# Output projection and second feed-forward moved to token-major groups with seven products for eight

## The chip, the cores and the metric

The kernel runs on one core of a Trainium2 chip. The metric is the time of one execution in device microseconds (us). TensorE (PE) multiplies, VectorE (DVE), ScalarE (ACT) and GpSimd (POOL) do the rest, and SyncE (SP) issues the loads.

## What is computed

Two transformer blocks in float32 on 256 tokens of width 2048. The first mixes two attentions, multiplies by `w_out`, and has a gated feed-forward (FFN) of inner width 5632. The second runs gated linear attention beside differential attention, multiplies by `w_o`, and has an FFN with a causal convolution over three tokens. Cut to what the change touches:

```python
h = h + mixed @ w_out
hn = rmsnorm(h, ffn_norm)
h = h + (silu(hn @ w_gate) * (hn @ w_up)) @ w_down
x = rmsnorm(h, final_norm)                        # the second block's input
m = token_mixer(rmsnorm(x, attn_pre_norm))        # ends with o @ w_o
x = x + rmsnorm(m, attn_post_norm)
up = rmsnorm(x, ffn_pre_norm) @ w_ffn_in          # 2048 -> 2 * 5632
a, b = up[..., :5632], up[..., 5632:]
a = conv3(a) + conv_b                             # three taps over tokens
f = (gelu(a) * b) @ w_ffn_out
out = x + rmsnorm(f, ffn_post_norm)
```

## The kernel before

Every product is made of split operands: a float32 value is cut into a high part (ACT copies and rounds, line L471 for weights) and a low part (DVE subtracts, L475), and high·high, high·low and low·high are summed in PSUM. Weights stream through SP (L421) in pieces of 128x1024; a few pieces are held split ahead of use (`look`).

There are two forms of product.

- **Channel-major** (`group_w`, `mm_w`, L513 to L517): the weight tile stands in the array, the 256 tokens move. For each 128x128 weight tile there is one matmul of 512 columns (high weight, the tokens' high and low parts side by side) and one of 256 columns (low weight). I call the two a pair. The result has channels on the partitions.
- **Token-major** (`group_t`, L597): 128 tokens stand, 512 weight columns move, three matmuls of 512 columns per product. The result has tokens on the partitions. Here two pairs of k-tiles (k-tile: 128 rows of the weight) are not multiplied in the eight block products that two pairs of tiles need but in seven, of sums of blocks (Winograd's form of Strassen's scheme). The roles are B11, B22, t1, t3, t2, B21, t4; t1, t3, t2, t4 need a weight piece that DVE adds together first (L453), and t1, t3, t2 and B22 use sums of activation blocks (`combos`). The other k-tiles (`std`) are multiplied as usual. After t4, `early` sums four PSUM banks (`sums`, L634 to L638); at the end `late` adds the other four.

Before the change the first block's `w_out` (2 groups), gate and up (11 groups) and `w_down` (6 groups in three parts) are token-major, from `block1_out` and `block1_ffn`. The second block's `w_o` (`block2_out`) and its FFN (`block2_ffn`) are channel-major: 256 pairs for `w_o`, 1408 for the first FFN matrix, 704 for the second.

At the end of `block1_ffn` the residual is transposed on PE eight blocks at a time (`turned`, L668), and for each block ACT and DVE make the split operand (L503, L504), ACT makes two squares for the two norms' statistics (L699), which POOL sums (L709), and ACT copies the residual (L1192). `block2_out` collects the statistics of the norm after `w_o` the same way; `norm_now` turns them into a factor by matmuls against ones, and then DVE and POOL scale and add 16 tiles (L1492, L1493), from which the operand of the FFN is split (L503, L504). In `block2_ffn`, `act` turns each pair of FFN columns into an operand: halves summed (L676, L679), scaled (L685), convolved (L1512, L1513, L1515), gelu (L1517), product (L1520), split (L500, L501). The end is a norm over channels again, 16 tiles and 16 stores (L1553 to L1555).

Order: the program is written as one stream of groups with side tasks. `tick` counts the estimated time of the matmuls issued, and every 2400 ns `pump` lets each side task (a generator) go one `yield` further. A layer under the kernel then sets each engine's final order; each engine runs its own in order. A token-major group calls `finish(*tasks)` ahead of t2, since the side task's transposes use the bank that t2 will use:

```python
if op == "t2":
    self.finish(*tasks)
...
if op == "t4" and not left["t2"]:
    early(b)
    self.one = self.map[ROLES["t3"]]
```

Of the kernel before, what the change touches and what calls it, by code (L numbers as in the profile page):

```python
# [17 lines left out]
P = 128  # L18
# [9 lines left out]
PARTS = ((0, 15), (15, 15), (30, 14))  # L28
PARTS_T = ((0, 16), (16, 16), (32, 12))
# [3 lines left out]
DOWN_PAIRS = ((0, 1), (2, 3))  # L33
UCOLS = 2048
# [27 lines left out]
def group_order(npairs, rest):  # L62

    rest, out = list(rest), []
# [10 lines left out]
def weight_plan():  # L75
# [13 lines left out]
    def tgroup(key, w, kts, pairs, col):  # L89
# [5 lines left out]
        c2 = [(col + 512, col + 1024)] if isinstance(w, str) else c1  # L95
# [9 lines left out]
        orders[key] = group_order(len(pairs), rest)  # L105
# [40 lines left out]
    for p, (i0, n) in enumerate(PARTS_T):  # L146
# [15 lines left out]
    for g in range(8):  # L162
        group(("wo", g), "w_o_2", list(range(8, 16)) + list(range(8)), [(256 * g, 256 * g + 256)])
    for p, (i0, n) in enumerate(PARTS):
        for i in range(i0, i0 + n):
            for c in range(2):
                kts = list(range(8 * c, 8 * c + 8))
                ra, rb = [(128 * i, 128 * i + 128)], [(FF + 128 * i, FF + 128 * i + 128)]
                unit(("fi", i, c), ("w_ffn_in_2", kts, ra + rb))
        for g in range(8):  # L170
            group(("fo", p, g), "w_ffn_out_2", range(i0, i0 + n), [(256 * g, 256 * g + 256)])
# [119 lines left out]
class Prog:  # L291
# [69 lines left out]
    def tmp(self, tag="tmp", bufs=6):  # L361
        return self.ring.tile([P, S], F32, tag=tag, name=tag, bufs=bufs)
# [267 lines left out]
    def sums(self, b):  # L630

        nc = self.nc
        e, v, w, c = [self.fz.tile([P, 512], F32, tag="ft", name="ft", bufs=4) for _ in range(4)]
# [5 lines left out]
        return e, w, v, c  # L639
# [4 lines left out]
    def residual(self, h, g):  # L644

        nc = self.nc
        at = [h[t][:, 1024 * g + 512 * m:1024 * g + 512 * m + 512] for t in range(2) for m in range(2)]

        def early(b):
            for a, x in zip(at, self.sums(b)):  # L650
# [6 lines left out]
        return early, late  # L657

# [89 lines left out]

    def norm_now(self, acc, last, n, first, warm=(0, 0, 0)):


        nc = self.nc
        ss = self.bank("ms")
        sq = self.square(last)
        if warm[0]:
            self.keep_warm(warm[0])
        for i, a in enumerate((acc, sq)):
            for t in range(2):
                nc.tensor.matmul(ss[:, t:t + 1], a[:, t * P:t * P + P], self.ones[:, 0:1],
                                 start=(i == 0 and t == 0), stop=(i == 1), skip_group_check=True)  # L760
        r = self.rsqrt(self.mean_eps(ss[:, 0:2], n))
        if warm[1]:
            self.keep_warm(warm[1])
        b = self.bank("ms")
        rB = self.bcast(r, bank=b, first=lambda: [
            nc.vector.tensor_tensor(x, x, b[:, :S], op=ALU.mult) for x in first])
        if warm[2]:
            self.keep_warm(warm[2])
        return rB
# [130 lines left out]
    def block1_mix(self):  # L900
# [175 lines left out]
        for j in range(16):  # L1076
# [13 lines left out]
            for a, b in OUT_PAIRS:  # L1090
                if j == b:
                    cm.append(self.combos(gates[a][0], za, self.cbp))
        return mixed, cm

    def block1_out(self, mixed, cm):
# [6 lines left out]
        ss = self.hp.tile([P, 2, 4], F32, name="ss")  # L1102

        def done(j, src):
            hn.append(self.hl(src, self.col("ffn_norm", j)))
            for i, p in enumerate(GU_PAIRS):
                if j in p:
# [3 lines left out]
                    if all(k in xg for k in p):  # L1111
                        cs.append(self.combos(xg[p[0]], xg[p[1]], self.hp))

        task = None
        for g in range(2):
            early, late = self.residual(h, g)
            self.group_t(("out", g), mixed, cm, OUT_PAIRS, early, late, [task] if task else ())
            for t in range(2):
                for m in range(2):
                    at = slice(1024 * g + 512 * m, 1024 * g + 512 * m + 512)  # L1120
# [556 lines left out]
```

## Time and profile before

| what | value |
|---|---|
| median of 3 runs | 2526.42 us (2525.63 to 2526.6) |
| the profiled execution's own time | 2526.12 us |
| its span in the profile | 2524.3 us |
| PE busy | 2485.4 us, 98% |
| DVE busy | 1842.0 us, 73% |
| ACT busy | 1372.8 us, 54% |
| POOL busy | 118.2 us, 5% |
| moved by DMA | 458.46 MB, 182 GB/s on average |

The span is what the profiler saw of the program; the execution's own time lies 1.8 us above it. A busy PE is not a PE at its best: matmuls overlap, and a matmul's shown length (some 390 ns for 512 columns) is longer than the step from one to the next. So counts of matmuls in a stretch of time say more than busy shares.

### The profile page before, as it was taken

The numbers are of one execution on the slowest core, as the hardware profiler recorded it, in microseconds if no ns is written. First come the engines' busy times: TensorE is split into PE (matmuls) and PEld (weight loads), VectorE is DVE, ScalarE is ACT, GpSimd is POOL, SyncE is SP. The second block draws the span as 40 slices with busy tenths as digits, with TensorE's granted clock in tenths as the row PEclk, the third lists the DMA queues.
The fourth block names the chain that finished last, engine by engine and source line by source line (L and its number), as shares of the span: only waits on it lengthen the run. The fifth ranks groups of instructions, "written<-read, shape, count | busy, mean of one in ns | idle before, by whom it ended". The sixth has DMA issues, their size and how long they took to land.

```text
span 2524.3 us, 35146 instructions
## 1 busy us (share of the span) xinstructions
PE 2485.4 (98%) x13218; PEld 2128.2 (84%) x13218; DVE 1842.0 (73%) x2617; ACT 1372.8 (54%) x2036; POOL 118.2 (5%) x134
## 2 busy tenths in 40 slices
PE   9999999999999999999999999999999999999997
PEld 8988888888788888888888888887888888888886
DVE  8766775888887878878786677666876567656765
ACT  6555565556555455545465545555655455545553
POOL 3000000000000000000012000013000000000002
PEclk9999999999999999999999999999999999999998
DMA  6644555566556565656555544464555555555552
GB/s 235 200 159 142 167 176 184 188 212 199 193 183 208 184 205 179 201 188 206 182 184 163 187 158 151 144 203 146 175 188 183 193 189 190 183 191 191 187 174 92
DMA packets 131723, 458.46 MB, mean 182 GB/s; under 512 B 14624, under 2 KB 17056, under 8 KB 131296
## 3 DMA queue, kind: packets, MB, share of 16 engines
q1 hardware_dynamic: 130608, 452.78, 54.7%
q10 hardware_dynamic: 944, 3.43, 0.4%
q8 instruction: 103, 1.69, 0.3%
q14 instruction: 68, 0.56, 0.1%
HBM read 454.06 MB, written 2.10 MB: 181 GB/s over the span
## 4 chain that ended last, share of the span: by engine, by line
PE 94%; DVE 4%; ACT 1%; issue 1%; POOL 0%; DMA 0%; POOLq 0%; SPq 0%; ACTq 0%; DVEq 0%
PE acc L516 33%; PE q L597 30%; PE acc L517 17%; PE acc L514 3%; PE acc L549 2%; PE acc L548 2%; PE acc L550 2%; PE acc L513 1%; PE ms L789 1%; DVE wl L475 1%; PE tr L668 1%; DVE hl L504 1%; PE ms L1337 1%; PE ms L818 1%; ACT wh L471 0%
## 5 line engine op out<-in xcount | busy, mean ns | idle before, releaser
L475 DVE TENSOR_TENSOR wl<-raw,wh 128x1024 fp32r<-128x1024 f32 (+4 forms) x939 | 1116.1, 1196 | 499.8 <-ACT wh L471 495.8
L471 ACT ACTIVATE wh<-raw 128x1024 fp32r<-128x1024 f32 (+4 forms) x939 | 968.2, 1033 | 748.1 <-PE acc L516 344.7
L516 PE MATMUL acc<-hl,wh 128*128 128x512 f32 x3746 | 1327.2, 396 | 8.3 <-DVE hl L504 6.5
L517 PE MATMUL acc<-hl,wl 128*128 128x256 f32 x3746 | 1048.4, 281 | 0.6 <-DVE wl L475 0.5
L516 PEld LDWEIGHTS acc<-hl,wh 128*128 128x128 f32 x3746 | 703.2, 188 | 168.2 <-DVE hl L504 6.4
L517 PEld LDWEIGHTS acc<-hl,wl 128*128 128x128 f32 x3746 | 707.0, 189 | 9.1 <-DVE wl L475 1.9
L597 PE MATMUL q<-wh,hl 128*128 128x512 f32 x1988 | 624.3, 392 | 0.0
L597 PEld LDWEIGHTS q<-wh,hl 128*128 128x128 f32 x1988 | 372.2, 188 | 80.4 <-ACT wh L471 0.4
L597 PE MATMUL q<-wl,hl 128*128 128x512 f32 x994 | 389.8, 392 | 1.5 <-DVE wl L475 1.5
L597 PEld LDWEIGHTS q<-wl,hl 128*128 128x128 f32 x994 | 186.5, 188 | 42.1 <-DVE wl L475 2.3
L676 ACT ACTIVATE ev<-acc 128x256 f32<-128x256 f32 x288 | 106.3, 384 | 182.5 <-PE acc L514 181.3
L709 POOL TENSOR_TENSOR ssq<-ssq,sq 128x256 f32<-128x256 f32 x77 | 73.8, 967 | 1531.0 <-ACT sq L699 1529.1
L679 DVE TENSOR_TENSOR tmp<-acc,ev 128x256 f32<-128x256 f32 x257 | 101.5, 423 | 60.0 <-ACT ev L676 59.8
L514 PE MATMUL acc<-hl,wh 128*128 128x512 f32 x288 | 108.2, 396 | 0.0
L597 PE MATMUL q<-wh,combo 128*128 128x512 f32 x304 | 101.4, 395 | 0.0
L548 PE MATMUL acc<-wh,hl 128*128 128x512 f32 (+4 forms) x264 | 93.8, 357 | 1.9 <-ACT hl L503 1.4
L453 DVE TENSOR_TENSOR raw<-raw 128x1024 f32<-128x1024 f32 x76 | 93.0, 1224 | 1.9
L549 PE MATMUL acc<-wl,hl 128*128 128x512 f32 (+4 forms) x264 | 91.0, 346 | 3.1 <-DVE wl L475 2.5
L550 PE MATMUL acc<-wh,hl 128*128 128x512 f32 (+4 forms) x264 | 89.5, 344 | 0.6 <-DVE hl L504 0.6
L513 PE MATMUL acc<-hl,wl 128*128 128x256 f32 x288 | 82.8, 287 | 0.0
L597 PEld LDWEIGHTS q<-wh,combo 128*128 128x128 f32 x304 | 57.1, 188 | 14.7 <-PE q L597 0.6
L597 PE MATMUL q<-wl,combo 128*128 128x512 f32 x152 | 60.0, 395 | 0.0
(275 smaller groups left out, 1625.6 us busy)
## 6 DMA issues: line engine op xcount, KB each, us to landing
raw<-in_w_dram SPq DMA_DIRECT2D x801, 512.0 KB, 4.4
raw<-in_w_dram SPq DMA_DIRECT2D x18, 384.0 KB, 3.6
raw<-in_w_dram SPq DMA_DIRECT2D x16, 362.0 KB, 4.0
raw<-in_w_dram SPq DMA_DIRECT2D x16, 346.0 KB, 3.6
raw<-in_w_dram SPq DMA_DIRECT2D x15, 256.0 KB, 3.8
raw<-in_w_dram SPq DMA_DIRECT2D x8, 364.0 KB, 3.7
raw<-in_w_dram SPq DMA_DIRECT2D x8, 348.0 KB, 3.7
x<-in_xT_dram SPq DMA_DIRECT2D x8, 256.0 KB, 5.7
```

The lines of the kernel that those rows point to most:

```text
L471: self.nc.scalar.activation(wh[:, :n], raw[:, :n], AF.Copy)
L475: self.nc.vector.tensor_tensor(wl[:, :n], raw[:, :n], wh[:, :n].bitcast(F32), op=ALU.subtract)
L513: nc.tensor.matmul(acc[:, S:], wl, x[:, 0, :], start=False, stop=False)
L514: nc.tensor.matmul(acc, wh, x, start=False, stop=True)
L516: nc.tensor.matmul(acc, wh, x, start=first, stop=False)
L517: nc.tensor.matmul(acc[:, S:], wl, x[:, 0, :], start=False, stop=last)
L548: nc.tensor.matmul(acc, xh, wh, start=(k == 0), stop=False)
L549: nc.tensor.matmul(acc, xh, wl, start=False, stop=False)
L550: nc.tensor.matmul(acc, xl, wh, start=False, stop=(k == n - 1))
L597: nc.tensor.matmul(b[r], x[i], w[j], start=left[r] == total[r], stop=left[r] == 1)
L676: nc.scalar.activation(e, acc[:, S:], AF.Copy)
L679: nc.vector.tensor_tensor(out, acc[:, :S], e, op=ALU.add)
```

## The change

- `w_o` becomes 2 token-major groups, the first FFN matrix 11, the second 6 in three parts, each with two pairs of k-tiles in seven products (`WO_PAIRS`, `FI_PAIRS`, `FO_PAIRS`). The first group of the FFN starts with four usual k-tiles (`lead`) before its seven products.
- The residual stays token-major to the end. After the first block it is multiplied by `final_norm`'s gain where it stands, from a gain row broadcast to all partitions (`row`), and the statistics come from ACT's squares with a sum along the row (`squares`, `mean_of`), before and after the gain. No matmul against ones, no POOL sum and no copy of the residual is left there.
- After `w_o`: squares, one factor per token, 14 small matmuls (`keep_warm`), gains, then per 512 columns two updates of the residual, two squares, eight transposes and four split operands (`operand`).
- In the FFN, after each group ACT scales four 128x512 tiles, and four times: four transposes, an ACT copy of 128x512, ACT, DVE, DVE, ACT, DVE for convolution, gelu and product, then the split (`gated`).
- The end: squares, factor, eight updates of 128x512 and eight stores.

```diff
-PARTS = ((0, 15), (15, 15), (30, 14))
-PARTS_T = ((0, 16), (16, 16), (32, 12))
+PARTS = ((0, 16), (16, 16), (32, 12))
...
+WO_PAIRS = ((0, 1), (2, 3))
+FI_PAIRS = ((4, 5), (6, 7))
+FO_PAIRS = ((0, 1), (2, 3))
...
-    for g in range(8):
-        group(("wo", g), "w_o_2", list(range(8, 16)) + list(range(8)), [(256 * g, 256 * g + 256)])
+    for g in range(2):
+        tgroup(("wo", g), "w_o_2", list(range(8, 16)) + list(range(8)), WO_PAIRS, 1024 * g)
...
+        for g in range(i0 // 4, (i0 + n) // 4):
+            tgroup(("fi", g), "w_ffn_in_2", range(16), FI_PAIRS, 512 * g, FF + 512 * g, 0 if g else 4)
+        for g in range(2):
+            tgroup(("fo", p, g), "w_ffn_out_2", range(i0, i0 + n), FO_PAIRS, 1024 * g)
...
+    def squares(self, src, ss):
+
+        sq = self.fz.tile([P, 512], F32, tag="sq", name="sq", bufs=1)
+        self.nc.scalar.activation(sq, src, AF.Square, accum_out=ss)
...
+                    gain = self.row(0, g)
+                    for i, a in enumerate(self.blocks(h, g)):
+                        at = slice(2 * g + i % 2, 2 * g + i % 2 + 1)
+                        self.squares(a, sa[:, i // 2, at])
+                        nc.vector.tensor_tensor(a, a, gain[:, 512 * (i % 2):512 * (i % 2) + 512], op=ALU.mult)
+                        self.squares(a, sb[:, i // 2, at])
 
                     def done(i, s, g=g):
-                        nonlocal sa, sb
-                        j = 8 * g + i
-                        x2.append(self.hl(s, self.gfp[:, j:j + 1]))
-                        sa = self.stat_add(sa, s)
-                        sb = self.stat_add(sb, s, self.col("final_norm", j))
-                        r = self.resp.tile([P, S], F32, tag="res", name="res", bufs=16)
-                        nc.scalar.activation(r, s, AF.Copy)
-                        hs.append(r)
+                        x2.append(self.hl(s, self.col("attn_pre_norm_2", 8 * g + i)))
...
+    def block2_out(self, ys, cw, h, n1):
...
+        for t in range(2):
+            nc.scalar.activation(h[t], h[t], AF.Copy, scale=n1.r[:, t:t + 1])
+        self.look, self.ahead = 3, True
+        for g in range(2):
+            gain = self.row(1, g)
+            early, late = self.residual(m, g, new=True)
+            self.group_t(("wo", g), ys, cw, WO_PAIRS, early, late)
...
+            if g:
+                r = self.rsqrt(self.mean_of(ss))
+                self.keep_warm(14)
...
+        def operand():
+            for c in range(4):
+                at = slice(512 * c, 512 * c + 512)
+                for t in range(2):
+                    nc.vector.scalar_tensor_tensor(h[t][:, at], m[t][:, at], r[:, t:t + 1], h[t][:, at],
+                                                   op0=ALU.mult, op1=ALU.add)
+                for t in range(2):
+                    self.squares(h[t][:, at], sx[:, t, c:c + 1])
+                yield from self.turned([h[t][:, at] for t in range(2)], 4, lambda i, x: done(4 * c + i, x), 0)
+            nx.r = self.rsqrt(self.mean_of(sx))
...
+        def gated(g, res, acts, ca):
+
+            for i in (0, 2, 1, 3):
+                nc.scalar.activation(res[i], res[i], AF.Copy, scale=nx.r[:, i // 2:i // 2 + 1])
+            yield
+            yield
+            ys = {}
+            for i in range(4):
+                b = self.bank("tr")
...
+                        nc.tensor.transpose(b[:, o:o + P], res[2 * t + m][:, P * i:P * i + P], self.cst("ident"))
+                au = self.tail.tile([P, 512], F32, tag="au", name="au", bufs=2)
+                nc.scalar.activation(au, b, AF.Copy)
...
+                nc.scalar.activation(y, y, AF.Gelu_apprx_tanh)
+                nc.vector.tensor_tensor(y, u, y, op=ALU.mult)
...
+                self.group_t(("fi", g), xn, cs, FI_PAIRS, lambda b: res.extend(self.sums(b)), late, [task])
+                task = self.add(gated(g, res, acts, ca), urgent=True)
+                task.step()
...
+            for g in range(2):
+                gain = self.row(2, g) if last else None
+                early, late = self.residual(f, g, new=p == 0)
+                self.group_t(("fo", p, g), Acts(acts, n), ca, FO_PAIRS, early, late, [task])
...
+        for c in range(4):
+            for t in range(2):
+                at = slice(512 * c, 512 * c + 512)
+                nc.vector.scalar_tensor_tensor(f[t][:, at], f[t][:, at], r[:, t:t + 1], h[t][:, at],
+                                               op0=ALU.mult, op1=ALU.add)
+                nc.sync.dma_start(self.t["out"][:, t * D + 512 * c:t * D + 512 * c + 512], f[t][:, at])
```

Three places show how the instructions stand now. First DVE in the FFN, of the kernel before, one pair of columns (`tmp`, `aux`: the halves summed and the activation; `wl`: low part of a weight piece; `hl`: split operand):

```order
L679 TENSOR_TENSOR tmp<-acc,ev 128x256 x2
L685 TENSOR_TENSOR aux<-tmp,rB 128x256 x2
L475 TENSOR_TENSOR wl<-raw,wh 128x1024
L1513 SCALAR_TENSOR_TENSOR aux<-aux,cc 128x255
L1515 SCALAR_TENSOR_TENSOR aux<-aux,cc 128x254
L475 TENSOR_TENSOR wl<-raw,wh 128x1024
L1520 TENSOR_TENSOR aux<-aux 128x256
L501 TENSOR_TENSOR hl<-aux,hl 128x256
```

And of the change, DVE from the late sums of one group into the next (`ft`: a group's sums; `y`, `au`: convolution and transposed copy; `raw`: a weight piece added up for t4):

```order
L1540 TENSOR_TENSOR ft<-q,ft 128x512 x2
L475 TENSOR_TENSOR wl<-raw,wh 128x1024 x4
L1518 SCALAR_TENSOR_TENSOR y<-au,cc,y 128x255
L475 TENSOR_TENSOR wl<-raw,wh 128x1024
L1520 SCALAR_TENSOR_TENSOR y<-au,cc,y 128x254
L1518 SCALAR_TENSOR_TENSOR y<-au,cc,y 128x255
L453 TENSOR_TENSOR raw<-raw 128x1024
L1523 TENSOR_TENSOR y<-au,y 128x256
L1520 SCALAR_TENSOR_TENSOR y<-au,cc,y 128x254
L475 TENSOR_TENSOR wl<-raw,wh 128x1024
L501 TENSOR_TENSOR hl<-y,hl 128x256
```

The convolution moved from between two weight pieces of a steady stream to the start of the next group, where the pieces for the seven products stand as well; two blocks are in work at once.

Second PE at the same place in the change, the third and fourth transposed block and the start of t2 (`tr`: transposed tiles; `q`: a product's bank; `combo`: sums of activation blocks):

```order
L1511 MATMUL tr<-cc,ft 128x128 x4
L597 MATMUL q<-wl,hl 128x512
L597 MATMUL q<-wh,hl 128x512 x2
L597 MATMUL q<-wl,hl 128x512
L597 MATMUL q<-wh,hl 128x512 x2
L597 MATMUL q<-wl,hl 128x512
L597 MATMUL q<-wh,hl 128x512 x2
L597 MATMUL q<-wh,combo 128x512
```

Eleven or so products stand between two blocks' transposes, and about ten between the fourth and t2; before, there was no transpose in this FFN.

Third DVE between `w_o` and the FFN. Of the kernel before (`mres`: a tile of the mixer's result, `res`: the residual, `rB`: the factor):

```order
L732 TENSOR_SCALAR small<-ms 128x2
L741 TENSOR_SCALAR dg<-cc,small 128x128 x2
L766 TENSOR_TENSOR mres<-mres,ms 128x256 x2
L1493 TENSOR_TENSOR res<-res,mres 128x256 x2
L1492 TENSOR_TENSOR mres<-mres,rB 128x256
L504 SCALAR_TENSOR_TENSOR hl<-res,cc,hl 128x256 x2
L1493 TENSOR_TENSOR res<-res,mres 128x256 x3
```

Of the change (`m_`: the mixer's result, `h_`: the residual, two tiles of 128 tokens each):

```order
L662 TENSOR_TENSOR m_15215<-q,m_15215 128x512 x2
L1464 TENSOR_TENSOR m_15214<-m_15214,row 128x512 x2
L1464 TENSOR_TENSOR m_15215<-m_15215,row 128x512
L674 TENSOR_REDUCE small<-ss 128x2
L1464 TENSOR_TENSOR m_15215<-m_15215,row 128x512
L756 TENSOR_SCALAR small<-small 128x2
L475 TENSOR_TENSOR wl<-raw,wh 128x1024
L1480 SCALAR_TENSOR_TENSOR h_5509<-m_15214,small,h_5509 128x512
L1480 SCALAR_TENSOR_TENSOR h_5510<-m_15215,small,h_5510 128x512
L1480 SCALAR_TENSOR_TENSOR h_5509<-m_15214,small,h_5509 128x512
L1480 SCALAR_TENSOR_TENSOR h_5510<-m_15215,small,h_5510 128x512
L504 SCALAR_TENSOR_TENSOR hl<-tr,cc,hl 128x256
```

The factor no longer passes through matmuls and a broadcast; instead four gains, a weight piece and four updates stand ahead of the first split operand.

## Rows read from the trace of the kernel before

**Rows 1.** The page: PE's busy time, and the chain that ended last, by engine.
```profile
PE 2485.4 (98%) x13218; PEld 2128.2 (84%) x13218; DVE 1842.0 (73%) x2617; ACT 1372.8 (54%) x2036; POOL 118.2 (5%) x134
...
PE 94%; DVE 4%; ACT 1%; issue 1%; POOL 0%; DMA 0%; POOLq 0%; SPq 0%; ACTq 0%; DVEq 0%
```

**Rows 2.** Windows by stage: stretch and its length, busy us (count) per engine, clock, DMA.
```profile
522.10:1329.20 807.10, 805.18 (x3575) 656.93 (x3574) 662.98 (x743) 440.25 (x529) 14.65 (x15) 1.00 0.59 195
1657.00:1746.90 89.90, 89.90 (x532) 79.47 (x531) 47.31 (x56) 50.78 (x83) 14.81 (x14) 1.00 0.57 189
1746.90:1754.70 7.80, 5.55 (x51) 5.39 (x49) 6.12 (x12) 3.49 (x8) 2.77 (x4) 1.00 0.80 258
1754.70:2503.90 749.20, 744.29 (x4250) 650.37 (x4250) 497.63 (x736) 390.35 (x593) 30.93 (x33) 1.00 0.54 177
2503.90:2524.30 20.40, 2.24 (x13) 1.80 (x12) 13.18 (x25) 1.13 (x3) 9.25 (x11) 0.56 0.31 103
```

**Rows 3.** Windows, PE alone: token-major products without transposes, then channel-major pairs.
```profile
830.00:910.00 80.00, 80.00 (x351) 1.00 0.64 211
...
1950.00:2050.00 100.00, 100.00 (x574) 1.00 0.59 193
```

**Rows 4.** Timeline of PE round four transposes: start, length, instruction; then all 88 grouped.
```profile
1013.58 0.62 PE L597 MATMUL q<-wh,hl 128*128 128x512 f32 x2
1014.03 0.60 PE L668 MATMUL tr<-cc,z 128*128 128x128 f32 x4
1014.39 0.48 PE L597 MATMUL q<-wl,hl 128*128 128x512 f32 x1
1014.70 0.63 PE L597 MATMUL q<-wh,hl 128*128 128x512 f32 x2
...
L668 PE MATMUL tr<-cc,z 128*128 128x128 f32 x88 | 13.3, 273 | 0.0
```

**Rows 5.** Groups of DVE and ACT in 522 to 1329: busy, mean ns, idle before.
```profile
L475 DVE TENSOR_TENSOR wl<-raw,wh 128x1024 fp32r<-128x1024 f32 x351 | 423.9, 1223 | 129.4 <-ACT wh L471 128.6
...
L1169 DVE TENSOR_TENSOR ft<-q,ft 128x512 f32<-128x512 f32 x44 | 28.3, 683 | 0.0
...
L1146 DVE SCALAR_TENSOR_TENSOR z<-ft,small,z 128x512 f32<-128x512 f32 x22 | 16.4, 746 | 0.0
...
L1122 ACT ACTIVATE sq<-h 128x512 f32<-128x512 f32 x8 | 5.0, 623 | 2.0 <-DVE h L655 2.0
```

**Rows 6.** Waits of PE in 522 to 1329: all of them.
```profile
PE q L597 <- DVE wl L475: 1.5, 2, 1.2
PE tr L668 <- ACT res L1192: 0.3, 1, 0.3
```

**Rows 7.** Groups of DVE and ACT in the second block's FFN.
```profile
L1513 DVE SCALAR_TENSOR_TENSOR aux<-aux,cc 128x255 f32<-128x255 f32 x44 | 21.0, 478 | 0.1
...
L1520 DVE TENSOR_TENSOR aux<-aux 128x256 f32<-128x256 f32 x44 | 18.5, 420 | 0.0
...
L500 ACT ACTIVATE hl<-aux 128x256 fp32r<-128x256 f32 x44 | 18.4, 417 | 54.8 <-DVE aux L1520 54.8
```

**Rows 8.** Windows, PE alone, after the first block's last product.
```profile
1329.00:1340.00 11.00, 10.13 (x62) 1.00 0.45 140
1340.00:1350.00 10.00, 8.59 (x41) 0.83 0.46 146
1350.00:1360.00 10.00, 7.24 (x39) 1.00 0.36 124
1360.00:1370.00 10.00, 9.26 (x60) 1.00 0.41 133
```

**Rows 9.** Timeline of ACT there: first operand of two successive transposed banks.
```profile
1342.98 0.47 ACT L503 ACTIVATE hl<-tr,gfp 128x256 fp32r<-128x256 f32 x1 [0.31 <-PE tr L668]
...
1348.23 0.46 ACT L503 ACTIVATE hl<-tr,gfp 128x256 fp32r<-128x256 f32 x1
```

**Rows 10.** Timeline at the end of the program.
```profile
2505.41 0.70 POOL L727 TENSOR_TENSOR small<-small,mhalf 128x2 f32<-128x2 f32 x1 [4.15 <-DVE small L732]
...
2520.61 0.42 DVE L1554 TENSOR_TENSOR mres<-mres,res 128x256 f32<-128x256 f32 x1
```

More of the change, by code (lines that the diff above doesn't have):

```diff
@@ L628, in group_t, with sums @@
         self.one = self.map[ROLES["t2"]]
-    def sums(self, b):
+    def sums(self, b, to=None):
         nc = self.nc
-        e, v, w, c = [self.fz.tile([P, 512], F32, tag="ft", name="ft", bufs=4) for _ in range(4)]
+        e, w, v, c = to or [self.fz.tile([P, 512], F32, tag="ft", name="ft", bufs=4) for _ in range(4)]
         nc.scalar.activation(e, b["B11"], AF.Copy)
@@ L747, in bcast @@
         return out
[L749 to L769, printed above, removed]
     def norm(self, res, acc, n, wait=0):
@@ L1101, in block1_out @@
         hn, cs, xg = [], [], {}
[L1102 removed]
+        ss = self.ring.tile([P, 2, 4], F32, name="ss", tag="ss", bufs=4)
         def done(j, src):
@@ L1134, in block1_ffn @@
         nc = self.nc
-        hs, x2, sa, sb = [], [], None, None
+        x2 = []
+        sa, sb = [self.ring.tile([P, 2, 4], F32, name="ss", tag="ss", bufs=4) for _ in range(2)]
         self.look, self.ahead = 4, True
@@ L1448, in block2_mix @@
         self.finish_all()
[L1449 to L1451 removed]
+        return yd + yg, cw
+    def block2_out(self, ys, cw, h, n1):
         nc = self.nc
[L1455 to L1470 removed]
@@ new lines, in block2_out @@
+        m = self.m
+        ss, sx = [self.ring.tile([P, 2, 4], F32, name="ss", tag="ss", bufs=4) for _ in range(2)]
+        for t in range(2):
[5 more added lines that the diff above has]
+            self.group_t(("wo", g), ys, cw, WO_PAIRS, early, late)
+            at = self.blocks(m, g)
+            for i in self.LATE_IN:
+                self.squares(at[i], ss[:, i // 2, 2 * g + i % 2:2 * g + i % 2 + 1])
+            if g:
+                r = self.rsqrt(self.mean_of(ss))
+                self.keep_warm(14)
+            for i in range(4):
+                nc.vector.tensor_tensor(at[i], at[i], gain[:, 512 * (i % 2):512 * (i % 2) + 512], op=ALU.mult)
@@ new lines, in block2_out, with done @@
+        xn, cs, xg = [], [], {}
+        def done(j, src):
+            xn.append(self.hl(src, self.col("ffn_pre_norm_2", j)))
+            for p in FI_PAIRS:
+                if j in p:
+                    xg[j] = self.tail.tile([P, S], F32, tag="xg", name="xg", bufs=3)
+                    nc.scalar.activation(xg[j], src, AF.Copy, scale=self.col("ffn_pre_norm_2", j))
+                    if all(k in xg for k in p):
+                        cs.append(self.combos(xg[p[0]], xg[p[1]], self.fz))
```

272 lines of the change are left out of this document (104 added, 168 removed).

## The prediction

> **What bounds the kernel now.** I read the page's busy times and chain first, then windows by stage, then the rate of products in windows of PE alone, and last the waits and timelines at the seams. PE is busy 98% of the span, and 94% of the chain that ended last is PE; no other engine reaches 74% [rows 1]. So the time is PE's list of matmuls times their step, plus the few places where PE waits. The windows show where those are: the two long stages run without holes, while 7.8 us lie between `w_o` and the FFN and 20.4 us behind the last product [rows 2]. A third place is the handover behind the first block's last product, where PE gets only 39 to 41 matmuls through in 10 us [rows 8]. I cost the change in the profiled execution (2526.12 us); the median of the runs, 2526.42, is 0.3 above it.
>
> **Products.** Before, the second block has 256 + 1408 + 704 = 2368 pairs. In steady channel-major work 574 matmuls, or 287 pairs, take 100 us: 0.3482 us a pair [rows 3], so 824.6 us in all. The stages last 89.9 + 749.2 = 839.1 [rows 2]; the other 14.5 us are taken up below.
>
> After, 17 groups of 16 k-tiles have 186 products each (192 less 6 for seven in place of eight) and two groups of 12 have 138: 3438 matmuls of 512 columns. Without transposes 351 of these take 80 us: 0.228 us each [rows 3], and 3438 take 783.9. This gains **40.7 us**. Two causes stand in it: 114 products fewer at 0.228 are 26.0; the other 14.7 come from the layout, since a pair's columns cost 1.5 × 0.228 = 0.342 us in tiles of 512, 0.0062 less than now, 2368 times.
>
> The second cause is where a rule can be weighed. The rows give 0.348 us for a pair and 0.228 for a product, both at a granted clock of 1.00 (2.4 GHz) [rows 3]. The Trainium skill (TensorE: Matmul & The Clock Gate, "Back-to-back issue gap") gives 518 cycles for 512 columns and 262 for 256, so, as an estimate from that page, 325.0 ns for a pair and 323.8 for one and a half products: the layout would save 3 us in place of 14.7, and the whole change about 9 us. The trace disagrees with both figures of that page, and with the pair more.
>
> This kernel already holds the new stage once: the first block's token-major stage has the same matrix sizes, groups and pairs, thus the same 3438 products, and with 136 transposes lasts 807.1 us [rows 2]. That is the check on the sum below.
>
> **Transposes.** New on PE's path are four 128x128 transposes per block: 4 blocks in 11 FFN groups (176) and 8 blocks for the FFN's operand (32), 208 in all. In the timeline four transposes start at 1014.03, the next product at 1014.39 and the one behind at 1014.70: they take a step of 0.36 us, and the next step is 0.31 in place of 0.23, so some 0.44 for four, 0.11 each [rows 4]. **+22.9 us**. One shows a length of 273 ns [rows 4]; by that they would cost 57 us, if they did not overlap, which I keep as a bound.
>
> **What is left in the stages.** Before, 14.5 us lie beside the pairs' steady rate, 13.8 of them in the FFN (749.2 less 2112 × 0.3482). After, the first block's stage tells what such a stage leaves: 807.1 − 783.9 − 136 × 0.11 = 8.2, with PE waiting in only two places, 1.8 us [rows 6]. To 8 I add two things that that stage doesn't have:
>
> - *The chain ahead of t2.* Per FFN group the four blocks must be convolved and transposed before t2, since t2 takes their bank. PE stands at t2 after 6 + 18 + 36 = 60 products and 16 transposes: 13.7 + 1.8 = 15.5 us. DVE's queue from the late sums to the last block's taps that free a buffer (`au` has two) is 4 sums at 0.68, 7 low parts at 1.22, one weight sum of like size, and six convolution steps at 0.478 plus three products at 0.42 [rows 5, 7]: some 16.6 us, begun about 1 us before the group's end, and ACT's gelu and copy, about 0.5 each, follow. With a part of these beside each other that is 0.6 to 1.1 us late; I take 0.6 for each of 11 groups, **6.6 us**. The ends are 0 (DVE a bit ahead, as in the first block's stage) and 2.9 (ACT and DVE alternating with both queues full). A wider bound comes from the same chain now: ACT waited 54.8 us over 44 blocks, 1.25 each, for DVE's gated product [rows 7]; paid four times a group that is 5 us.
> - *The FFN's start.* Before t2 of the first group PE has 48 + 60 products and 32 transposes, 28 us; from the first update to the last operand DVE has about 36 us of work (weight parts, updates, splits, the first sums of activation blocks), and begins 3 us ahead: **4 us**, ends 0 and 8.
>
> So 8 + 4 + 6.6 = 18.8 against 14.5: **+4.3 us**.
>
> **DVE as a bound.** A group of the FFN gives DVE 19 weight low parts and 4 weight sums at 1.22, 8 PSUM sums at 0.68, and four times 0.478 + 0.48 + 0.42 + 0.42: 40.7 us [rows 5, 7], against PE's 186 × 0.228 + 16 × 0.11 = 44.2. That is 92%; in the first block's stage it was 82% [rows 2]. PE hides it, except in the up to three groups where sums of activation blocks (about 3.7 us) come on top and both engines are level. I cost these at nothing; without cover it is a few us. POOL, busy 31 us in the FFN now [rows 2], loses its tensor work. The three gain rows, 512 KB each for a half, are loaded long ahead on queues that run at 54 to 64% [rows 2, 3]: nothing.
>
> **From `w_o` to the FFN.** Now 7.8 us [rows 2]. After: a late sum 0.68, its square 0.62, the power 0.70 on POOL, one weight low part 1.22 that stands in DVE's queue, four updates at 0.746, transposes 0.4, a split 0.47 [rows 4, 5, 9, 10], and, as an estimate, 1.9 for small sums and handing over between engines: 9.0. **+1.2 us**, ends −2 and +4.
>
> **The end.** Now 20.4 us, from statistics through matmuls, the power at 2505.41, and 16 tiles to DVE's last at 2520.61 [rows 2, 10]. After: sum, square and power as above 2.0, two gains of 0.7, eight updates at 0.746 = 6.0 [rows 5], 3.3 us from DVE's last end (2521.03) to the span's end as now [rows 10], and 2.6 for small sums and handing over: 15.3. **−5.1 us**, ends −8 and 0.
>
> **The handover from the first block.** From 1340 to 1370 PE starts 140 matmuls, where its last 10 us alone have 60 [rows 8]: about 40 slots, 6.7 us, are lost. The reason stands in ACT's timeline: successive transposed banks begin 5.25 us apart (1342.98, 1348.23), each with two tiles [rows 9], as each tile needs a split, two squares and a copy there. After, ACT does only the split, about 1 us a bank, but ahead of it stand eight squares at 0.62 [rows 5] and DVE's gains, and behind it two scalings of 128x2048 (some 2 us each, an estimate from ACT's half-size passes). I take **−3 us**, ends −7 and +4.
>
> **Sum.** −40.7 + 22.9 + 4.3 + 1.2 − 5.1 − 3 = **−20.4 us**. The profile becomes 2505.7, the median **2506 us**. The check: the first block's stage plus 72 more transposes (7.9), chain and start (10.6) gives 825.6; today's two stages are 839.1. The same −13.5 as the first three terms.
>
> **Rivals.**
>
> 1. *The chain ahead of t2 becomes the bound* (slower). `finish` lets t2 wait until all four blocks are through a ring of two `au` buffers and one bank, with ACT's scaling, copy and gelu and DVE's taps in turn, each behind weight work. For it: DVE at 92%, and ACT's 1.25 us per block in the same chain now [rows 7]. At 5 us a group it costs 55 in place of 6.6: 2554 us. The gain is gone at (20.4 + 6.6) / 11 = 2.5 us a group, and it is slower beyond doubt from 2.9. Against: the weights are held several pieces ahead, so DVE's taps needn't stand behind all low parts, and the first block's stage with the same t2 lost 1.8 us in all [rows 6]. Chance 0.08.
> 2. *The products gain less, or the seams nothing*: the layout saves 3 us and the handover 0, the rest as in the sum: 2506 + 11.7 + 3, about 2521; with either alone 2509 to 2518. Against: the first block's 807.1 us [rows 2]. Chance 0.17, a third of it within 5 us of the time before.
> 3. *Everything hides*: no wait ahead of t2 (−6.6), none at the start (−4), the handover whole (−4): about 2491. For it: the first block's stage waits 1.8 us in all [rows 6]. Chance 0.15.
> 4. *Transposes at full length*: 208 × 0.273 = 57 us, 34 above my term, 2540 us. The Trainium skill (TensorE: Matmul & The Clock Gate, "Part 4: PE-mode transpose") gives about 275 ns in a kernel and says they don't count as busy for the clock; the length agrees with the row's 273, the lost clock doesn't show. Against: a product starts 0.36 us behind four of them [rows 4], and the clock of the stage that holds 136 was 1.00 [rows 2]. Chance 0.02.
> 5. *The change doesn't do what it says*: the instructions do stand there (3438 more products of 512 columns, 208 more transposes, no pair in the second block), so I give it nothing.
>
> **Numbers.** My forecast has 0.58. A measurement of this kernel can tell about 0.2%, 5 us, from no change. Faster by more: the forecast, rival 3 and most of rival 2, **0.82**; within: **0.08**; slower: rivals 1 and 4, **0.10**. The range runs from 2494, short of rival 3's end, to 2524, which takes in rival 2 and a chain at 2.2 us a group; rivals 1 and 4 lie outside.
>
> **What the new profile would show.** Second-block windows with 351 products per 80 us between transposes; a span of four transposes near 0.4 us; PE's waits at t2 on ACT or DVE near 0.6 us per FFN group (2.5 or more would make the prediction wrong); DVE near 90% in the FFN; a tail near 15 us; about 9 us from `w_o` to the FFN; more than 50 matmuls in every 10 us of the handover. A first group that waits over 8 us, or a clock under 1.00 in the FFN, would also upset the sum.

## The result and the profile after

The changed kernel takes 2494.25 us (2494.12 to 2494.76, 4 runs) where the kernel before, beside it, took 2526.03 (2525.42 to 2526.6): a ratio of 0.9875, 95% interval 0.9858 to 0.9892, or 31.8 us less. I had said 2506, 20 less, with a range of 2494 to 2524. It is faster, and it lies inside the range, but only 0.25 us above its lower end. The profiled span fell from 2524.3 to 2492.4 us, by 31.9.

The page of the changed kernel, busy times and chain, answering to [rows 1]:

```profile
PE 2464.3 (99%) x12044; PEld 2061.7 (83%) x12044; DVE 1988.5 (80%) x2662; ACT 1431.6 (57%) x2006; POOL 38.4 (2%) x46
...
PE 96%; DVE 2%; ACT 1%; issue 0%; DMA 0%; POOL 0%; POOLq 0%; DVEq 0%; SPq 0%; ACTq 0%
```

PE is still what bounds the kernel, more than before. Its windows by stage (from the first block's last product: the handover and the mixer, `w_o`, the gap, the FFN, the end; columns as in [rows 2]):

```profile
1328.56:1652.42 323.86, 320.36 (x1857) 283.41 (x1856) 222.61 (x381) 179.58 (x291) 9.71 (x12) 0.99 0.50 161
1652.42:1737.76 85.34, 85.34 (x374) 69.75 (x373) 65.63 (x71) 45.86 (x56) 0.00 (x0) 1.00 0.70 233
1737.76:1746.99 9.23, 4.63 (x33) 3.77 (x31) 8.30 (x15) 5.09 (x13) 1.59 (x1) 0.82 0.34 123
1746.99:2479.66 732.67, 730.60 (x3270) 595.63 (x3270) 627.29 (x771) 453.54 (x598) 1.61 (x1) 1.00 0.55 183
2479.66:2492.40 12.74, 0.16 (x1) 0.00 (x0) 8.75 (x16) 1.80 (x6) 0.69 (x1) 0.69 0.44 165
```

Set against [rows 2], stage by stage:

| stage | before | after | difference | forecast |
|---|---|---|---|---|
| up to the first block's last product | 1329.2 | 1328.56 | −0.6 | 0 |
| handover and mixer | 327.8 | 323.86 | −3.9 | −3 |
| `w_o` and FFN | 89.9 + 749.2 | 85.34 + 732.67 | −21.1 | −13.5 |
| gap between them | 7.8 | 9.23 | +1.4 | +1.2 |
| the end | 20.4 | 12.74 | −7.7 | −5.1 |
| sum | | | −31.9 | −20.4 |

The sign was right in every stage that I had forecast to move. The change gained 11.5 us more than forecast; 7.6 of them lie in `w_o` and the FFN, and that is what most of the runs are about. All the waits of PE in that FFN:

```profile
PE q L597 <- ACT hl L503: 1.3, 3, 0.6
PE q L597 <- DVE hl L504: 0.8, 1, 0.8
PE q L597 <- ACT combo L573: 0.5, 1, 0.5
```

All five stand at its start, where operands are still being made. None is a wait of t2 for the bank of the transposes. DVE is busy 627.3 of 732.7 us there, 86%, and hidden as forecast.

### The profile page after: what moved, and what is told of

It reads as the page before. It is cut to its first block, busy times and chain, and to the rows that moved or that the text cites. A ratio compares the mean times of both kernels' runs of the same rounds, so it can differ in the third digit from the quotient of the medians.

```text
span 2492.4 us, 32676 instructions
## 1 busy us (share of the span) xinstructions
PE 2464.3 (99%) x12044; PEld 2061.7 (83%) x12044; DVE 1988.5 (80%) x2662; ACT 1431.6 (57%) x2006; POOL 38.4 (2%) x46
## 4 chain that ended last, share of the span: by engine, by line
PE 96%; DVE 2%; ACT 1%; issue 0%; DMA 0%; POOL 0%; POOLq 0%; DVEq 0%; SPq 0%; ACTq 0%
PE q L597 63%; PE acc L516 14%; PE acc L517 7%; PE acc L550 2%; PE acc L549 2%; PE acc L548 2%; PE acc L514 1%; PE ms L791 1%; PE tr L692 1%; PE tr L1511 1%; PE acc L513 1%; PE ms L1329 1%; PE ms L820 1%; DVE wl L475 0%; ACT wh L471 0%
## 5 line engine op out<-in xcount | busy, mean ns | idle before, releaser
L475 DVE TENSOR_TENSOR wl<-raw,wh 128x1024 fp32r<-128x1024 f32 (+3 forms) x988 | 1178.1, 1203 | 386.6 <-ACT wh L471 382.3
L471 ACT ACTIVATE wh<-raw 128x1024 fp32r<-128x1024 f32 (+3 forms) x988 | 1026.8, 1043 | 796.3 <-PE q L597 556.5
L597 PE MATMUL q<-wh,hl 128*128 128x512 f32 x3976 | 1253.8, 393 | 2.0 <-ACT hl L503 1.3
L597 PEld LDWEIGHTS q<-wh,hl 128*128 128x128 f32 x3976 | 745.2, 188 | 165.1 <-ACT hl L503 2.4
L597 PE MATMUL q<-wl,hl 128*128 128x512 f32 x1988 | 779.3, 392 | 0.3 <-DVE wl L475 0.3
L516 PE MATMUL acc<-hl,wh 128*128 128x512 f32 x1558 | 555.9, 399 | 1.0 <-ACT wh L471 0.6
L597 PEld LDWEIGHTS q<-wl,hl 128*128 128x128 f32 x1988 | 373.6, 188 | 80.7 <-DVE wl L475 0.7
L517 PE MATMUL acc<-hl,wl 128*128 128x256 f32 x1558 | 435.1, 281 | 0.7 <-DVE wl L475 0.7
L516 PEld LDWEIGHTS acc<-hl,wh 128*128 128x128 f32 x1558 | 292.1, 188 | 67.0 <-issue 2.1
L517 PEld LDWEIGHTS acc<-hl,wl 128*128 128x128 f32 x1558 | 293.4, 189 | 5.8 <-DVE wl L475 2.0
L453 DVE TENSOR_TENSOR raw<-raw 128x1024 f32<-128x1024 f32 x152 | 185.9, 1223 | 3.7
```

What stands on the lines that cost most here:

```text
L453: self.nc.vector.tensor_tensor(raw[:, :n], parts[a][:, :n], parts[b][:, :n], op=ALU.add)
L471: self.nc.scalar.activation(wh[:, :n], raw[:, :n], AF.Copy)
L475: self.nc.vector.tensor_tensor(wl[:, :n], raw[:, :n], wh[:, :n].bitcast(F32), op=ALU.subtract)
L516: nc.tensor.matmul(acc, wh, x, start=first, stop=False)
L517: nc.tensor.matmul(acc[:, S:], wl, x[:, 0, :], start=False, stop=last)
L597: nc.tensor.matmul(b[r], x[i], w[j], start=left[r] == total[r], stop=left[r] == 1)
```

## Experiments

Times here are medians; the kernel before, run beside them each time, took 2525.6 to 2526.4. I take no difference of medians under 2 us as shown. In the profiles two stretches of unchanged code differ by some 2 us from one profile to the next: the handover with the mixer (321.7 to 324.8 us) and the FFN's first group of 186 products. Much of this goes with how long the granted clock is low there (below). The rest repeats much better: from the 187th product of the FFN to its last, the three profiles with the same code there (the changed kernel, the later lambda task, more small matmuls) take 681.9, 681.9 and 681.8 us. I call this stretch the FFN behind its first group; differences in it can be told to a few tenths.

### Eight products again

```diff
-WO_PAIRS = ((0, 1), (2, 3))
-FI_PAIRS = ((4, 5), (6, 7))
-FO_PAIRS = ((0, 1), (2, 3))
+WO_PAIRS = FI_PAIRS = FO_PAIRS = ()
```

(and the late sums become copies where no early ones exist; `finish` is called ahead of the sixth k-tile, which is behind 60 products, about where t2 stood).

> The changed kernel without seven products in the second block: all k-tiles as usual, 192 and 144 products per group, no sums of weight pieces, no sums of activation blocks. My theory: PE's list sets the time, so 114 products more at 0.228 us, 26.0 us more than the changed kernel: 2520.3 us, 6 us under the kernel before; that rest is layout (-14.7), transposes (+22.9) and the seams. Rival, seven products pay less since their DVE sums hold PE up now and then: 10 to 18 us more, about 2508. Rival, the layout saves 3 us only: cannot be told from this run alone, but then the result would be near or above the kernel before only if the seams gained less than 10 us.

Measured: 2516.03 us (2513.72 to 2516.65), 21.8 more than the changed kernel; ratio to the kernel before 0.9956 (0.9941 to 0.9971). Its `w_o` and its FFN:

```profile
1653.73:1741.63 87.90, 87.90 (x385) 71.99 (x384) 47.29 (x50) 39.11 (x48) 0.00 (x0) 1.00 0.63 212
...
1750.86:2502.03 751.17, 751.04 (x3372) 614.86 (x3372) 438.11 (x528) 394.49 (x518) 0.69 (x1) 1.00 0.53 177
```

`w_o` grew by 2.56 us for 12 products, 0.213 each, and the FFN by 18.5 for 102, 0.181 each: the seven products paid 21.8 us and not 26.0. That is about midway between the two theories, 4.2 us under mine and 3.8 over the upper end of the rival. DVE's load fell from 86 to 58%, and PE's step, worked out next, got shorter by no more than 0.0008 us.

The run also bears on the layout. Both stages together last 839.1 us, just as before the change. Take off the 204 transposes in the FFN at 0.11 (22.4) and a slow start (2.3 us of slow clock and 0.6 of waits for operands, estimated from PE's timeline of this run), and 3552 products have 813.8 us, 0.2291 each. The 2368 pairs would take 824.6 us at the steady step of my sum. At their mean step over a longer stretch of the kernel before, 1718 pairs in 600 us, they would take some 827:

```profile
1800.00:2400.00 600.00, 600.00 (x3436) 1.00 0.58 189
```

The layout thus gains some 11 to 13 us where I had 14.7. The 3 us that I had estimated from the Trainium skill (TensorE: Matmul & The Clock Gate, "Back-to-back issue gap") are out by this run: the trace's pair at 0.348 us is dearer than the 325 ns worked out from that page, and the difference is real time.

The changed kernel by the same account: 818.0 less 22.4 less a start of 5.2 (worked out below) leave 790.4 us for 3438 products, 0.2299 each. So the 26 us for 114 products lose 2.3 at the start, where PE waits for operands and sums of activation blocks, and about 3 to a step longer by 0.0008.

### Each transpose twice

```diff
-                        nc.tensor.transpose(b[:, o:o + P], res[2 * t + m][:, P * i:P * i + P], self.cst("ident"))
+                        for _ in range(2):
+                            nc.tensor.transpose(b[:, o:o + P], res[2 * t + m][:, P * i:P * i + P], self.cst("ident"))
```

> Each of the 176 transposes in the FFN's groups is issued twice (same result). My theory: a transpose costs its step, 0.09 us when it follows another, so 176 x 0.09 = 15 to 176 x 0.11 = 19 us more: 2510 to 2514 us, PE's clock stays at 1.00. Rival, a transpose costs its shown length of 0.27 us: 48 us more, 2542 us.

Measured: 2514.64 us (2512.07 to 2515.44), 20.4 more, or 0.116 us for each of 176. The FFN in a window, and the transposes grouped:

```profile
1746.16:2499.95 753.79, 751.66 (x3446) 617.25 (x3446) 629.53 (x772) 458.08 (x598) 1.62 (x1) 0.99 0.53 177
```

```profile
L1512 PE MATMUL tr<-cc,ft 128*128 128x128 f32 x352 | 45.8, 272 | 0.0
```

The FFN grew by 21.1 us. Of these, 18.5 lie behind its first group (700.4 us against 681.9), where all 176 new transposes stand: 0.105 us each. The other 2.6 lie in the first group, whose code is unchanged but for its surroundings; there the granted clock was 0.57 from 1745 to 1753 us and 0.66 from 1765 to 1770. So a transpose's shown length is 272 ns and it costs 0.105: the term of the sum, 0.11 each, was right, and rival 4 has fallen. The mean clock of the whole stretch is 0.99, with 352 transposes in it.

### A longer chain ahead of t2

Three runs lengthen the chain from the late sums to the last transposed copy, on which t2 waits: one more ACT pass of 128x512 per block, one more DVE pass, four more ACT passes.

```diff
                 nc.scalar.activation(au, b, AF.Copy)
+                nc.scalar.activation(au, au, AF.Copy)
```

```diff
                 nc.scalar.activation(au, b, AF.Copy)
+                nc.vector.tensor_copy(au, au)
```

```diff
                 nc.scalar.activation(au, b, AF.Copy)
+                for _ in range(4):
+                    nc.scalar.activation(au, au, AF.Copy)
```

> One more ACT pass of 128x512 (the transposed copy onto itself) per block in the chain ahead of t2; ACT's load in the FFN goes from 62% to about 66%. My theory: the chain ends within 0 to 1 us of t2 now, so 0.5 us per block, 1 to 2 us per group, show as waits of PE at t2: 10 to 20 us more, 2504 to 2514 us. Rival, the chain has several us to spare: within 2 us of the changed kernel.

> One more DVE pass of 128x512 per block (the transposed copy onto itself), in the same place of the chain; DVE's load in a usual FFN group goes from 92% to about 97%. My theory: as with ACT's pass, 1.5 to 2.5 us per group, since the chain stands at t2's edge: 16 to 28 us more, 2510 to 2522 us, with PE's waits at t2. Rival, DVE's 8% to spare take it: within 2 us of the changed kernel.

> Four more ACT passes of 128x512 per block in the chain ahead of t2, about 2.2 us per block, 9 us per group. My theory after the run with one pass more (3.3 us in all): the order of PE moves usual products ahead of t2 when the chain gets longer, a part of the group's 96 later products, so a longer chain is hidden for some us more: 5 to 30 us more than the changed kernel. Rival, the edge is reached and each further us of chain is a wait: 11 x 7 to 9 = 75 to 100 us more.

Measured: 2497.52 us (2496.12 to 2497.86), 2498.29 (2496.72 to 2499.36) and 2503.69 (2500.91 to 2506.22): 3.3, 4.0 and 9.4 us more. Both first expectations were wrong, theory and rival: there are neither 10 to 28 us of waits nor none at all. (ACT's pass took 0.63 us and DVE's 0.42, so 2.5 and 1.7 us a group.) The expectation for four passes held: 9.6 us more of ACT's work in each of 11 groups cost 9.4 us in all, under 1 us a group.

What takes it up is seen in one FFN group of the profiles. These windows of PE alone (length, busy, matmuls, clock, DMA share, GB/s) run from the group's first product with sums of blocks to t2, in the changed kernel, with one ACT pass more, and with four:

```profile
2063.12:2078.31 15.19, 15.19 (x75) 1.00 0.62 210
```

```profile
2063.70:2079.32 15.62, 15.62 (x78) 1.00 0.63 207
```

```profile
2065.31:2084.98 19.67, 19.61 (x94) 1.00 0.61 205
```

PE is busy in all of them: it doesn't wait for t2, it does 16 transposes and 58, 60 and 77 products first (the windows also count matmuls that overlap their edges). In program order 54 products stand there. Over the 11 groups I count 54 to 58 in the changed kernel, 55 to 63 with one pass, 72 to 88 with four. The layer that sets the engines' final order moves t2 back behind usual products of the same group, of which 96 stand behind t4, until the chain is through. Its end can be seen in the same group: ACT's copy of the last transposed bank, and t2, of the changed kernel and of the one with four passes:

```profile
2077.68 0.58 ACT L1513 ACTIVATE au<-tr 128x512 f32<-128x512 f32 x1
2078.31 0.50 PE L597 MATMUL q<-wh,combo 128*128 128x512 f32 x1
...
2084.14 0.59 ACT L1513 ACTIVATE au<-tr 128x512 f32<-128x512 f32 x1
2084.98 0.40 PE L597 MATMUL q<-wh,combo 128*128 128x512 f32 x1
```

The sum over the groups of what PE's step exceeds 0.23 us ahead of t2, beside transposes left out, is about 1.5 us in the changed kernel and 0.9 in the one with four passes. In the latter PE pays elsewhere, waiting for weights that ACT's longer queue makes late (L475 3.9 us, L471 1.2 us in its waits behind 1780 us). In its profile four such waits between 2455 and 2464 us, 4.3 us together, go with a low granted clock, where the changed kernel has 1.00:

```profile
2462.00:2470.00 8.00, 7.25 (x21) 0.57 0.72 223
```

Both are part of what this run lost; its profile took the longest of its four runs, 2506.22 us. With one pass of ACT more PE waits 1.8 us for weights (L475).

### The seams

Three edits for what the profile after still shows. The second block's small lambda task later:

```diff
         def lambdas():
+            for _ in range(10):
+                yield
```

> The second block's lambda task (two small products, a mask load of DVE, two matmuls, an exponential with its table load of ACT) begins ten side-task steps, some 24 us, later. My theory: in the handover these small instructions stand at the head of PE's, DVE's and ACT's queues behind the norm's two powers (PE waits 1.65 us at L1250, DVE about 1 us for the masks, ACT 1.28 us for the table), so the handover gets 3 to 5 us shorter: 2489 to 2491 us. Rival, the handover waits for the squares, gains and splits alone: within 1 us of the changed kernel.

The first FFN group without seven products and without `lead` (with the copies of the first run, and with `finish` ahead of the 14th k-tile):

```diff
-            tgroup(("fi", g), "w_ffn_in_2", range(16), FI_PAIRS, 512 * g, FF + 512 * g, 0 if g else 4)
+            tgroup(("fi", g), "w_ffn_in_2", range(16), FI_PAIRS if g else (), 512 * g, FF + 512 * g)
```

> The first group of the second FFN without seven products: 192 usual products in the order of the operands, no sums of weight pieces in it. My theory: PE's waits at its start (3.4 us for operands and sums of activation blocks) go, 6 products more cost 1.4: 2 us less, 2492 us. Rival, the waits move behind other operands, since DVE has 36 us of work before the last of them either way: 1 to 3 us more than the changed kernel.

And PE kept at work in the gap:

```diff
-                self.keep_warm(14)
+                self.keep_warm(30)
```

> 30 in place of 14 small matmuls between w_o and the FFN, alone. From the run with three edits, where the gap was 9.0 in place of 9.2 us and the FFN's start had its full step: 2 us less than the changed kernel, 2492 us, all of it in the first 10 us of the FFN. Rival: the gain there was the first group's, and this one changes nothing.

All three together:

> Both of these together, and 30 in place of 14 small matmuls between w_o and the FFN. My theory: PE has no matmul from 1741.1 to 1745.0 and the granted clock is 0.50 from 1745 to 1749, so that the first nine products take 0.43 us each; with small matmuls through the gap they take 0.23 and the four transposes 0.4 in place of 2.0, together 3 us; with the other two 7 to 10 us less than the changed kernel: 2484 to 2487 us. Rival, the small matmuls' added length delays the first transposes as much as the clock gives back: no gain in the gap, 2487 to 2490 us.

Measured: lambda later 2492.25 us (2490.89 to 2493.75), first group 2492.94 (2492.45 to 2494.81), more small matmuls 2492.19 (2490.11 to 2493.88): each 1.3 to 2.1 us under the changed kernel, at the edge of what can be told. The lambda task stayed 1.3 short of its theory, the first group 0.9 short, and the small matmuls came out at the number expected, though not where I had put it (below). All three: **2487.83 us** (2487.77 to 2488.25), 6.4 us under it, ratio to the kernel before 0.9848 (0.9835 to 0.9861). That beats both kernels, and is 0.8 us above the range of its theory, in that of its rival.

The reason for the third edit stands in PE's timeline of the changed kernel (start, length, instruction, what it waited for):

```profile
1737.76 3.29 PE L718 MATMUL ms<-ones 128*128 128x128 f32 x28
1744.96 1.47 PE L692 MATMUL tr<-cc,h 128*128 128x128 f32 x4 [3.92 <-DVE h L1480]
1746.99 0.80 PE L597 MATMUL q<-wh,hl 128*128 128x512 f32 x1 [0.56 <-ACT hl L503]
1747.59 0.63 PE L597 MATMUL q<-wl,hl 128*128 128x512 f32 x1
1748.02 1.05 PE L597 MATMUL q<-wh,hl 128*128 128x512 f32 x2
```

After 28 short matmuls PE stands still for 3.9 us, and the FFN's first products take steps of 0.43 us where they take 0.23 later. PE's windows from 1740 on, of the changed kernel and of the one with 30:

```profile
1740.00:1745.00 5.00, 1.08 (x11) 0.87 0.41 152
1745.00:1749.00 4.00, 3.31 (x9) 0.50 0.01 3
1749.00:1753.00 4.00, 4.00 (x18) 0.81 0.00 0
```

```profile
1740.00:1745.00 5.00, 4.66 (x43) 1.00 0.46 147
1745.00:1749.00 4.00, 3.01 (x14) 1.00 0.03 11
1749.00:1753.00 4.00, 4.00 (x21) 1.00 0.00 0
```

The granted clock stood at 0.50, the lower of its two levels (1.2 GHz), and with PE at work through the gap it stays at the upper. From 1745 to 1753 us that is 8 matmuls more, 1.8 us. But in the profile of this edit alone the FFN still lasts 732.54 us (732.67). PE's waits for operands at its start are no longer than they were, 2.6 and 2.7 us. What differs is the clock behind them, here from 1761 to 1769 us in the changed kernel, with 30 small matmuls, and with all three edits:

```profile
1761.00:1769.00 8.00, 6.02 (x28) 1.00 0.60 203
...
1761.00:1769.00 8.00, 6.38 (x21) 0.79 0.57 190
...
1761.00:1769.00 8.00, 8.00 (x40) 1.00 0.57 181
```

So in this profile the low clock took back, a few us later, what the full one had given in the gap. The four runs of the edit bear this out: the two with a mean granted clock of 0.998 took 2490.1 and 2491.0 us, the other two (0.996 and 0.997) 2493.4 and 2493.9, and the profile is of the longest. Since the changed kernel has the same waits there at a clock of 1.00, the waits alone don't say when it falls; that stays open. With the first group's edit PE doesn't wait there, and the time stays won: the FFN takes 730.61 us with that edit alone and 729.29 with all. From 1761 to 1768 us PE's steps exceed their usual length by 3.4 us in the changed kernel; with the 1.8 of the slow clock that makes the 5.2 used above, an estimate.

The handover, in PE's windows of the changed kernel, answering to [rows 8], and with the lambda task later:

```profile
1340.00:1350.00 10.00, 7.84 (x34) 0.72 0.37 118
1350.00:1360.00 10.00, 9.99 (x61) 0.94 0.24 69
1360.00:1370.00 10.00, 10.00 (x65) 1.00 0.73 233
```

```profile
1340.00:1350.00 10.00, 8.73 (x56) 1.00 0.28 92
1350.00:1360.00 10.00, 8.99 (x57) 1.00 0.40 131
1360.00:1370.00 10.00, 10.00 (x64) 1.00 0.79 256
```

The change gets 160 matmuls through in these 30 us where there were 140, and the later task 177. Handover and mixer fall from 323.86 to 321.04 us with it. The clock has a part in this: from 1340 to 1360 us it is 0.72 and 0.94 in the changed kernel and 1.00 with the later task, so the short queue and the upper clock can't be told apart here. In that run's profile the FFN took 735.02 us, 2.4 more than in the changed kernel, with the same code: all of it in the first group, where its clock was 0.73 from 1745 to 1753 us and 0.79 from 1761 to 1769.

### Why seven products paid 22 us and not 26

Of what is missing, the start has 2.3 us and the longer step 3. For the step, two runs take the suspects away. In the second block alone, plain operands in place of sums of activation blocks:

```diff
-                cmb = lambda m: (cs[c + i][:, 0, m, :], cs[c + i][:, 1, m, :])
+                if key[0] in ("wo", "fi", "fo"):
+                    cmb = lambda m: cut(xs[ka], t1 if m & 1 else t0)
+                else:
+                    cmb = lambda m: (cs[c + i][:, 0, m, :], cs[c + i][:, 1, m, :])
```

> In the second block the products of B22, t1, t2 and t3 take plain operands in place of the sums of activation blocks (which are still computed); the output is then another. It leaves the count of products, and DVE's and ACT's work, as they are. Open is why 114 products fewer gave 22 us and not 26, as the products' mean step is 0.230 us with sevens and 0.2285 without. If the operand of summed blocks is slow in itself (0.234 in its products), the FFN gets 3 to 5 us shorter: 2489 to 2491 us. If not, nothing changes: 2493 to 2496 us.

And no sums of weight pieces (the addition at L453 is skipped for the second block):

> In the second block no weight pieces are summed on DVE (t1, t3, t2 and t4 take one of the two pieces as it is; the output is then another); 76 DVE passes of 1.22 us go. If DVE's sums beside the products, or the weights coming late, make the step longer, the FFN and w_o get 3 to 5 us shorter: 2489 to 2491 us. If not, within 1 us of the changed kernel.

Measured: 2490.94 us (2489.19 to 2491.37) and 2493.35 (2493.04 to 2493.77). The first is 3.3 less, and its FFN 729.72 us, 2.95 less; but its handover and mixer, whose code is the same, were 2.2 shorter too, with a clock of 0.89 from 1340 to 1355 us against 0.77. Behind the first group, where equal code repeats to 0.1 us, its FFN takes 680.4 us against 681.9: 1.5 less. The second run is 0.9 less, and behind the first group it takes 682.4. So DVE's sums of weights aren't the reason. The products with summed blocks (0.234 us mean step in the changed kernel with the high weight, against 0.230 for plain ones) account for about half of the 3 us. Why their step is longer, and where the other half is, stays open.

## Why the prediction was right, point by point

- **Products**, 40.7 us: 26.0 for fewer products measured 21.8, and 14.7 for the layout some 11 to 13. Both were reckoned with the step 0.228 of [rows 3]; the stages' mean is 0.2299. 3438 products at 0.0019 are 6.5 us that I had counted as gain; they come up again in the third point. (287 pairs in 100 us are 0.3484 each and not 0.3482: 0.5 us more for the pairs, and as much less beside them, so the sum stays.)
- **Transposes**, +22.9: 208 at the 0.105 of the run are 21.8. Reading the step in [rows 4], not the length, was right.
- **What is left in the stages.** This is the term that was mis-sized. I put 18.8 us there, 8 + 4 + 6.6; the stages' 818.0 less 783.9 less 22.4 leave 11.7: 5.2 at the FFN's start (forecast 4, where 36 less 28 less 3 give 5, and of other make: 3.4 of operands and 1.8 of the clock, of which I hadn't thought), and 6.5 for the longer step, with the 1.5 us ahead of t2 in it, where the first block's stage had let me expect 8. The step that failed is "that is 0.6 to 1.1 us late; I take 0.6 for each of 11 groups, 6.6 us". The chain was about as long as I had said: in the group shown it runs from the first late sum at 2060.02 to the end of the last copy at 2078.26, and t2 starts 0.05 us later. But I held t2's place in PE's order fixed at 60 products, and it isn't: when the chain is late, the order puts usual products ahead of t2. The runs with one and four passes more show that by their counts. For the same reason rival 1 was much farther off than its 2.9 us a group let it seem: 9.6 us more chain cost under 1 us a group.
- **The check** by the first block's 807.1 us was the better half of the forecast: with 72 transposes at 0.105 and the 5.2 us of the start it gives 819.9, against the measured 818.0: without a term for the chain it would have been within 2 us.
- **DVE**, forecast near 90%, was at 86% of the FFN and stayed hidden, as costed.
- **The gap**, +1.2: +1.4. **The handover**, −3: −3.9, but not by the picture that was forecast. ACT's own work on a bank did fall to two splits of 0.47 us. Yet successive banks still begin 5.5 to 6.3 us apart, and ahead of the third ACT waits 3.1 us for PE:

```profile
1343.26 0.47 ACT L503 ACTIVATE hl<-tr,cc 128x256 fp32r<-128x256 f32 x1
...
1349.51 0.47 ACT L503 ACTIVATE hl<-tr,cc 128x256 fp32r<-128x256 f32 x1 [3.11 <-PE tr L692]
```

  And 34 matmuls in the window from 1340 us are far from the "more than 50 matmuls in every 10 us" that I named as a sign. The lambda task ahead of the banks and the clock of 0.72 stand there in place of ACT's copies and squares. That the size came out is in part luck.
- **The end**, −5.1: −7.7. The profile of the end:

```profile
2480.38 0.69 DVE L662 TENSOR_TENSOR m<-q,m 128x512 f32<-128x512 f32 x1
2480.98 1.28 DVE L1557 TENSOR_TENSOR m<-m,row 128x512 f32<-128x512 f32 x2
...
2483.16 0.69 POOL L751 TENSOR_TENSOR small<-small,mhalf 128x2 f32<-128x2 f32 x1 [720.99 <-DVE small L756]
2483.88 5.39 DVE L1561 SCALAR_TENSOR_TENSOR m<-m,small,h 128x512 f32<-128x512 f32 x8 [0.87 <-POOL small L751]
```

  Eight updates, overlapping a little, take 5.4 us and not 6.0. Three of the last four gains run while ACT squares or ahead of its sums; one, 0.68 us, stands between the last square and the factor. So half of the 1.4 us for gains, and about 1 us of the 2.6 for small sums and handing over, weren't paid.

The sum came out inside the range, but by 0.25 us, less than the spread of its four runs, so that it did is in part luck. The largest errors of the waits had one sign, as I took most unknowns on the side of a wait; the products' error had the other and offset 6.5 us of them. The result lies nearer to rival 3 (about 2491) than to my 2506: its "no wait ahead of t2" came true, but its FFN without a wait at the start and its whole handover didn't.

## What to carry to other kernels

A second stage like one that the kernel has already was forecast best here by that stage's own time; what is added to it should be only what the first stage demonstrably lacks. Before costing a wait on a chain that ends "at the edge", look whether the order of the waited-for engine is fixed: where a scheduler may put other work ahead of the wait, the price is what remains when that work has run out. Matmuls and transposes that follow each other are costed by the step between starts, not by their shown length: here a transpose cost 0.105 us and showed 0.272. Before two profiles are compared stage by stage, compare their granted clocks at the seams: 2 us of what looked like spread stood there. And where PE pauses for some us, look at the clock of the products behind the pause: keeping PE busy there cost nothing here, but in the profile with that edit alone the clock fell a few us later, where PE waited for operands, and the gain was gone.

## What was not expected of the hardware

Behind a pause of 3.9 us the granted clock was 0.50 in the stretch 1745 to 1749 us, with steps of 0.43 us in seven products; with 60 short matmuls in the same place (30 in the kernel, each two for PE) it was 1.00. With those it was 0.79 from 1761 to 1769 us, where no single pause of PE was over 0.8 us. Products of 512 columns ran at two paces, 0.68 and 0.70 us for three, that alternate within one stage at a clock of 1.00; over 163 windows of 4 us the pace did not follow the load of DVE or of the DMA (correlations 0.13 and 0.07) and only weakly that of ACT (0.4). What sets it stays open. DVE's copy of a 128x512 tile onto itself took 0.42 us, while a sum of that size with one operand out of PSUM took 0.68.
